# Squares of layer 0's norm on GpSimd, a new head of the program with constant dummies: a two-layer hybrid decoder trunk on one core

## The chip, the cores and the metric

One core of one Trainium2 chip. The metric is the device time of one execution in microseconds (us), the median of the runs. The engines are named as in the profile: PE (TensorE matmul), PEld (its weight loads), DVE (VectorE), ACT (ScalarE), POOL (GpSimd), SP (SyncE, which here issues nearly all DMAs). A name with a q behind it (ACTq, SPq) is the engine's instruction queue issuing a DMA.

## The reference, cut to what matters

Two layers over a sequence of 256 tokens of width 1024, batch 1, all in float32:

```python
def hybrid_layer(x, norm_w, w_in, ...):
    h = rmsnorm(x, norm_w)
    proj = jnp.matmul(h, w_in)          # 1024 -> 4360 columns
    ...                                  # attention (8 heads), retention (4), mLSTM (4), each gated
    y = jnp.concatenate([ya, yb, yc], axis=-1)
    return x + jnp.matmul(y, w_out)      # 1024 -> 1024
def reference(x, ...):
    for layer in range(2):
        x = hybrid_layer(x, ...)
    return rmsnorm(x, final_norm_w)
def rmsnorm(x, w):
    return x * lax.rsqrt(jnp.mean(x * x, axis=-1, keepdims=True) + 1e-6) * w
```

## The kernel before, in words

**Tiling.** x lies transposed in SBUF, width on the partitions: tile `px` holds 8 blocks (k = 0 to 7) of 128 partitions x 256 tokens, and beside them the small parameters. Float32 products are made from split operands: every operand is split into a high part (`hi`, `xh`: a copy of type fp32r) and a low part (`lo`, `xl`: the operand minus its high part), and each product takes three matmuls, high x high, high x low, low x high. The high part of a weight chunk is an ACT copy, the low part a DVE subtraction; for x (`split_x`, L431) the high part is an ACT copy scaled by the norm weight, the low part a DVE scalar_tensor_tensor. `xh` and `xl` lie in one tile, `xx`. The norm's 1/rms is not applied to x but to the results, when they leave PSUM.

**Staging.** The weights of a layer come in 21 chunks through three buffers of `raw`, `hi` and `lo` each (in the listings of an engine's order these are raw_85 to raw_87, hi_88 to hi_90, lo_91 to lo_93). Chunks 0 and 1 (`aq0`, `ak0`) are worked on together, block by block: for each k the matmuls are high/low of `xx` block k with both chunks, 12 matmuls per k, 4 groups of three; those 32 groups are the first real work of PE. `loader` (L390) issues their pieces on SP in the order x block, weight pieces, with five cuts of k (0; 1; 2, 3; 4, 5; 6, 7); the pieces of chunk 0 for k = 0 and k = 1 (the list `early`, L364) are issued on ACT's queue instead.

**Order of the work.** The kernel's own planner (`Sched`) sets each engine's order: every operation has an engine and a cost in the planner's clock, and what can start first is emitted first. Each engine then runs its list strictly in that order, waiting for semaphores where an operand isn't there. A `("act", 507.0, ...)` request is planned as ACT's work whatever engine its function really uses.

**The head of the program** (L359 to L377), emitted in front of everything the planner emits: DVE fills `ones`; ACT's queue issues the two early DMAs and then runs one Exp, in front of which the compiler puts the load of ACT's function table; DVE fills `mhalf`; POOL fills `va`, `vc`, `cpad` and the four padded tiles `zu` and `zd`; DVE zeroes a tile of `sb`, and PE runs two matmuls of 384 columns on it whose result nobody reads (dummies).

**The norm of a layer** (`norm`, L481): four Square operations on ACT, each over two blocks of x (128x512), into tiles `t`, summed by DVE; then a matmul with `ones` sums over the partitions, and POOL raises to the power -0.5. For layer 0 the third and fourth of these DVE sums stand in front of and between the low parts of the weight chunk 2, and the first one (`t_94<-t_94,t_95`) among the low parts of chunks 0 and 1.

Lines: L259 is every DVE operation, L265 every ACT operation of the planner, L280 every matmul, L288 every DMA that SP issues; they are told apart by tiles.

Of the kernel before, what the change touches and what calls it, by code (L numbers as in the profile page):

```python
# [55 lines left out]
W_TOTAL = W_OFFS[-1]  # L56


P_NW, P_CW, P_CB, P_GB, P_YW = 0, 16, 48, 56, 72
P_N = 72 + 8  # L60

T_ID, T_DIST, T_COS, T_SIN, T_QS, T_MC, T_DEC = 0, 128, 512, 768, 1024, 1028, 1412
T_1 = 1028
# [165 lines left out]
def trunk(ctx: ExitStack, tc: tile.TileContext, xp: bass.AP, w: bass.AP, fn: bass.AP,  # L229
# [7 lines left out]
    def sb_tile(shape, name, dt=F32):  # L237
        return cp.tile(shape, dt, name=name)
# [22 lines left out]
    def A(out, in_, func, after=None, table=False, **k):  # L261
        cost = _n(out) / 1.2 + 80 + 93 * sum(isap(v) for v in k.values())
        if func == AF.Ln or table:
            cost += 1283
        return op("act", cost, lambda: nc.scalar.activation(out, in_, func, **k), after)  # L265
# [21 lines left out]
    def D(cost, out, in_):  # L287
        return op("sp", cost, lambda: nc.sync.dma_start(out, in_))  # L288
# [14 lines left out]
        return wait(ev)  # L303


    px = sb_tile([128, P_N + KT * S], "px")
    pr = px[:, :P_N]
    x = px[:, P_N:].rearrange("p (k t) -> p k t", t=S)
    tb = sb_tile([128, T_N], "tb")
    ident = tb[:, T_ID:T_ID + 128]  # L310
    ones = sb_tile([128, 2], "ones")
# [44 lines left out]
    sc.pool("pj", [pp.tile([128, 512], F32, name=f"pj{i}") for i in range(4)])  # L356
    sc.pool("mx", [pp.tile([128, 512], F32, name=f"mx{i}") for i in range(4)])

    nc.vector.memset(ones, 1.0)  # L359

    early = []
    for k in range(2):
        d = slice(k * 256, (k + 1) * 256)
        early.append(nc.scalar.dma_start(sc.pools["raw"][0][0][0][:, d], w[:, d]))  # L364
    nc.scalar.activation(ones[:, 1:2], ones[:, 0:1], AF.Exp)
    nc.vector.memset(mhalf, -0.5)
    nc.gpsimd.memset(va, 1.0)
    nc.gpsimd.memset(vc, 1.0)
    nc.gpsimd.memset(cpad, 0.0)

    for tag, half in (("zu", slice(64, 128)), ("zd", slice(0, 64))):
        for t, _ in sc.pools[tag][0]:
            nc.gpsimd.memset(t[half].bitcast(F32), 0.0)
    dummy = sc.pools["sb"][0][0][0]
    nc.vector.memset(dummy, 0.0)
    for _ in range(2):
        nc.tensor.matmul(sc.pools["mx"][0][3][0][:, :384], dummy[:, :128], dummy, start=True, stop=True)  # L377

    evs = {}

# [9 lines left out]
    def loader():  # L390
        for i in range(NL):
            l, c = divmod(i, NW)
            n = W_SIZES[c]
            o = l * W_TOTAL + W_OFFS[c]
            if i == 1:
                continue
            t = yield acq("raw")
            raws[i] = t
            if i < 2:
                if i == 0:  # L400
                    t1 = yield acq("raw")
                    raws[1] = t1
                    for a, b in ((0, 1), (1, 2), (2, 4), (4, 6), (6, 8)):
                        o1, o2 = P_N + a * S if a else 0, P_N + b * S
                        e = yield D((o2 - o1) * 512 / 360.0, px[:, o1:o2], xp[:, o1:o2])
                        for k in range(a, b):
                            sc.set(E("x0", k), e + 1100)
                        for m in range(2):
                            if m == 0 and b <= 2:
                                e = yield op("sp", 364, lambda: early[a])  # L410
                            else:
                                e = yield D((b - a) * 364, (t, t1)[m][:, a * 256:b * 256],
                                            w[:, o + m * 2048 + a * 256:o + m * 2048 + b * 256])
                            for k in range(a, b):
                                sc.set(E("rawk", m, k), e + 1100)
                continue
            m = 2 if i == 2 else 1
            for j in range(m):
                a, b = j * n // m, (j + 1) * n // m
                e = yield D((b - a) * 512 / 360.0, t[:, a:b], w[:, o + a:o + b])  # L420
                for q in range(2 * j // m, 2 * (j + 1) // m):
                    sc.set(E("raw", i, q), e + 1100)
            if i == 2:
                e = yield D(1500, tb[:, :T_1], tab[:, :T_1])
                sc.set(E("tab"), e + 1100)
            if i == 4:
                e = yield D(3500, tb[:, T_1:], tab[:, T_1:])
                sc.set(E("tab2"), e + 1100)
        sc.spawn(last_in(), 2)

    def split_x(l, k):  # L431
        wk = pr[:, P_NW + l * 8 + k:P_NW + l * 8 + k + 1]
        yield A(xh[:, k, :], x[:, k, :], AF.Copy, scale=wk)
        t = yield V("scalar_tensor_tensor", xl[:, k, :], x[:, k, :], wk, xh[:, k, :].bitcast(F32),
                    op0=OP.mult, op1=OP.subtract)
        sc.set(E("x", l, k), t)
# [44 lines left out]
    def norm(l):  # L481

        ss = None
        for k in range(0, KT, 2):
            for z in (k, k + 1):
                yield wait(E("x0", z) if l == 0 else E("res", l - 1, z))
            sq = yield acq("t512")
            yield A(sq, x[:, k:k + 2, :].rearrange("p a t -> p (a t)"), AF.Square)
            if ss is None:
                ss = sq  # L490
            else:
                e = yield V("tensor_tensor", ss, ss, sq, op=OP.add)
                sc.release("t512", sq, e)
# [729 lines left out]
```

## Time and profile before

| | |
|---|---|
| time, median of 3 runs | 300.46 us (300.12 to 301.92) |
| the profiled execution, its own time | 299.76 us |
| its span, first to last instruction | 298.0 us |
| what lies around the span in it | 1.76 us |
| mean granted TensorE clock | 0.994 |
| busy: PE, DVE, ACT, POOL | 290.7, 257.9, 197.8, 13.7 us |

A row of a timeline gives the start (us from the span's start), the busy time, the engine, the line, the operation with its output and inputs, and how many instructions are merged in the row; in brackets the idle time before it and what ended it. Times of the matmuls' ends are modelled, so PE's pace is read from the distances between starts.

### The profile page before, as it was taken

The page shows a single profiled execution, that of the slowest core. Times are in us where ns is not written, and L with a number is a line of the kernel's source. Part 1 is how long each engine was busy: PE and PEld are TensorE (multiplying, and loading weights), DVE is VectorE, ACT ScalarE, POOL GpSimd, SP SyncE. Part 2 cuts the span into 40 slices and gives each one's busy share as a digit, 9 for nine tenths or more (in the row PEclk, how much of TensorE's full clock was granted, in tenths as well). Part 3 has the DMA queues.
Part 4 walks back from the last instruction along what each step waited for, and adds up shares of the span by engine and source line. Part 5 has one row for each costly group of instructions (what it writes and reads, how often), then busy time and mean ns, then how long its engine had stood idle before and what let it go on. Part 6 is the DMA issues. An engine that isn't in the chain of part 4 may idle for free.

```text
span 298.0 us, 4797 instructions
## 1 busy us (share of the span) xinstructions
PE 290.7 (98%) x1792; PEld 258.3 (87%) x1792; DVE 257.9 (87%) x551; ACT 197.8 (66%) x344; POOL 13.7 (5%) x17
## 2 busy tenths in 40 slices
PE   7999999999999999999999999999999999999992
PEld 5998999888989888899988888988899988888882
DVE  4969999999999997885779999999999999956553
ACT  7948997889358439644565799779555265745533
POOL 6000000000002002000020000000002002000000
PEclk9999999999999999999999999999999999999997
DMA  7999455664800560745317663446541624340003
GB/s 243 398 400 326 141 196 206 192 232 141 274 11 3 170 251 8 265 153 157 128 21 263 211 218 130 152 144 211 213 143 34 250 59 166 122 148 0 2 4 137
DMA packets 9095, 48.58 MB, mean 163 GB/s; under 512 B 1008, under 2 KB 1904, under 8 KB 4080
## 3 DMA queue, kind: packets, MB, share of 16 engines
q1 hardware_dynamic: 8784, 48.02, 46.4%
q8 instruction: 14, 0.23, 0.3%
q10 hardware_dynamic: 288, 0.26, 0.3%
q14 instruction: 9, 0.07, 0.1%
HBM read 47.23 MB, written 1.05 MB: 162 GB/s over the span
## 4 chain that ended last, share of the span: by engine, by line
PE 87%; DVE 9%; DMA 1%; ACT 1%; issue 1%; DVEq 0%
PE pj L280 69%; PE mx L280 14%; PE mx L285 4%; DVE lo L259 3%; DVE t L259 1%; DVE st L259 1%; DVE small L259 1%; DMA px<-xp 1%; DVE hc L259 1%; DVE sb L259 1%; DVE raw L259 1%; DVE et L259 0%; ACT raw L265 0%; DVE zd L259 0%; DVE zu L259 0%
## 5 line engine op out<-in xcount | busy, mean ns | idle before, releaser
L259 DVE TENSOR_TENSOR lo<-raw,hi 128x1024 fp32r<-128x1024 f32 (+2 forms) x96 | 102.7, 1087 | 7.9 <-ACT hi L265 7.7
L265 ACT ACTIVATE hi<-raw 128x1024 fp32r<-128x1024 f32 (+2 forms) x96 | 88.5, 946 | 9.7 <-DMA raw<-w 3.8
L280 PE MATMUL pj<-hi,xx 128*128 128x512 f32 (+1 forms) x320 | 94.3, 373 | 0.0
L280 PE MATMUL pj<-xx,hi 128*128 128x512 f32 (+1 forms) x272 | 88.0, 377 | 0.1
L280 PE MATMUL pj<-xx,lo 128*128 128x256 f32 x240 | 68.7, 286 | 0.0
L280 PEld LDWEIGHTS pj<-hi,xx 128*128 128x128 f32 x320 | 57.4, 188 | 9.0
L280 PE MATMUL pj<-lo,xx 128*128 128x512 f32 (+1 forms) x160 | 59.4, 371 | 0.0
L280 PEld LDWEIGHTS pj<-xx,hi 128*128 128x128 f32 x272 | 50.2, 194 | 9.6 <-ACT hi L265 1.3
L280 PEld LDWEIGHTS pj<-xx,lo 128*128 128x128 f32 x240 | 46.0, 192 | 0.1
L280 PEld LDWEIGHTS pj<-lo,xx 128*128 128x128 f32 x160 | 30.1, 188 | 4.5
L265 ACT ACTIVATE sb<-sb,small 128x128 f32<-128x128 f32 (+1 forms) x48 | 19.5, 449 | 4.9 <-DVE small L259 2.4
L265 ACT ACTIVATE t<-pj 128x256 f32<-128x256 f32 x26 | 9.8, 378 | 17.0 <-PE pj L280 16.9
L265 ACT ACTIVATE st<-t 64x512 fp32r<-64x512 f32 x26 | 16.1, 628 | 4.5 <-DVE t L259 4.1
L280 PE MATMUL pj<-yh,lo 128*128 128x256 f32 x56 | 15.9, 284 | 0.0
L280 PE MATMUL pj<-yh,hi 128*128 128x256 f32 x56 | 15.9, 284 | 0.0
L280 PE MATMUL pj<-yl,hi 128*128 128x256 f32 x56 | 15.8, 283 | 0.0
L1109 POOL TENSOR_TENSOR small<-small,mhalf 128x8 f32<-128x8 f32 x4 | 6.9, 1730 | 181.7 <-DVE small L259 181.7
L280 PE MATMUL mx<-st,st 128*128 128x128 f32 (+1 forms) x64 | 15.1, 270 | 0.0
L265 ACT ACTIVATE t<-pj,small 128x512 f32<-128x512 f32 (+1 forms) x12 | 7.3, 610 | 11.2 <-PE pj L280 11.1
L259 DVE TENSOR_TENSOR t<-pj,t 128x256 f32<-128x256 f32 x26 | 10.9, 419 | 2.2 <-ACT t L265 2.1
L265 ACT ACTIVATE t<-t 32x512 f32<-32x512 f32 (+1 forms) x20 | 12.6, 630 | 0.3
L280 PEld LDWEIGHTS mx<-st,st 128*128 128x128 f32 x64 | 12.1, 189 | 0.6
(151 smaller groups left out, 480.4 us busy)
## 6 DMA issues: line engine op xcount, KB each, us to landing
raw<-w SPq DMA_DIRECT2D x37, 1024.0 KB, 4.8
raw<-w SPq DMA_DIRECT2D x2, 1056.0 KB, 6.3
raw<-w SPq DMA_DIRECT2D x6, 256.0 KB, 5.0
raw<-w SPq DMA_DIRECT2D x2, 512.0 KB, 6.6
tb<-tab SPq DMA_DIRECT2D x1, 960.0 KB, 10.1
px<-xp SPq DMA_DIRECT2D x3, 256.0 KB, 4.3
tb<-tab SPq DMA_DIRECT2D x1, 514.0 KB, 7.5
raw<-fn SPq DMA_DIRECT2D x1, 512.0 KB, 3.2
```

The source lines that it names most:

```text
L259: return op("dve", cost, lambda: getattr(nc.vector, name)(out, *a, **k), after)
L265: return op("act", cost, lambda: nc.scalar.activation(out, in_, func, **k), after)
L280: return op("pe", cost, lambda: nc.tensor.matmul(out, a, b, start=start, stop=stop, skip_group_check=True), after)
L285: return op("pe", 110.0, lambda: nc.tensor.transpose(out, in_, idn))
L1109: yield G(1600, lambda: nc.gpsimd.tensor_tensor(vs, vs, mhalf[:, :8], op=OP.pow))
```

## The change

Six edits, all in the head of the program and in layer 0.

1. The four Squares of layer 0's norm become products x*x on POOL (`tensor_tensor`); the planner still books them as ACT's work of 507 ns. Layer 1 keeps ACT.
2. The high part of x block 0 in layer 0 (one 128x256 operation) goes from ACT to DVE (`tensor_scalar`); the planner still books it as ACT's.
3. The Exp that brings ACT's function table stands in front of ACT's two early DMA issues.
4. PE's dummies: eight matmuls of 128 columns on the constant zero tile that the framework fills at the program's start, in place of two of 384 columns on a tile that DVE zeroes. They stand at the top of the head.
5. POOL fills only the columns of `va`, `vc` and `cpad` that nothing else writes.
6. In `px` the norm weights (16 columns) lie in front of x and the other parameters behind it, so the first DMA of x has 272 columns in place of 336 and the last one 576 in place of 512.

```diff
@@ -56,8 +56,9 @@
 W_TOTAL = W_OFFS[-1]
 
 
-P_NW, P_CW, P_CB, P_GB, P_YW = 0, 16, 48, 56, 72
-P_N = 72 + 8
+P_NW, P_X = 0, 16
+P_CW = P_X + KT * S
+P_CB, P_GB, P_YW, P_N = P_CW + 32, P_CW + 40, P_CW + 56, P_CW + 64
 
 T_ID, T_DIST, T_COS, T_SIN, T_QS, T_MC, T_DEC = 0, 128, 512, 768, 1024, 1028, 1412
 T_1 = 1028
@@ -303,9 +304,9 @@
         return wait(ev)
 
 
-    px = sb_tile([128, P_N + KT * S], "px")
-    pr = px[:, :P_N]
-    x = px[:, P_N:].rearrange("p (k t) -> p k t", t=S)
+
+    pr = px = sb_tile([128, P_N], "px")
+    x = px[:, P_X:P_CW].rearrange("p (k t) -> p k t", t=S)
     tb = sb_tile([128, T_N], "tb")
     ident = tb[:, T_ID:T_ID + 128]
     ones = sb_tile([128, 2], "ones")
@@ -356,25 +357,23 @@
     sc.pool("pj", [pp.tile([128, 512], F32, name=f"pj{i}") for i in range(4)])
     sc.pool("mx", [pp.tile([128, 512], F32, name=f"mx{i}") for i in range(4)])
 
+    zero = nc.const_aps.tensor(0.0, (128, 128), F32)
+    for _ in range(8):
+        nc.tensor.matmul(sc.pools["mx"][0][3][0][:, :128], zero, zero, start=True, stop=True)
     nc.vector.memset(ones, 1.0)
+    nc.scalar.activation(ones[:, 1:2], ones[:, 0:1], AF.Exp)
 
     early = []
     for k in range(2):
         d = slice(k * 256, (k + 1) * 256)
         early.append(nc.scalar.dma_start(sc.pools["raw"][0][0][0][:, d], w[:, d]))
-    nc.scalar.activation(ones[:, 1:2], ones[:, 0:1], AF.Exp)
     nc.vector.memset(mhalf, -0.5)
-    nc.gpsimd.memset(va, 1.0)
-    nc.gpsimd.memset(vc, 1.0)
-    nc.gpsimd.memset(cpad, 0.0)
-
+    nc.gpsimd.memset(va[:, :, :, HD:], 1.0)
+    nc.gpsimd.memset(vc[:, :, :, HD:], 1.0)
+    nc.gpsimd.memset(cpad[:, :, :3], 0.0)
     for tag, half in (("zu", slice(64, 128)), ("zd", slice(0, 64))):
         for t, _ in sc.pools[tag][0]:
             nc.gpsimd.memset(t[half].bitcast(F32), 0.0)
-    dummy = sc.pools["sb"][0][0][0]
-    nc.vector.memset(dummy, 0.0)
-    for _ in range(2):
-        nc.tensor.matmul(sc.pools["mx"][0][3][0][:, :384], dummy[:, :128], dummy, start=True, stop=True)
 
     evs = {}
 
@@ -401,8 +400,8 @@
                     t1 = yield acq("raw")
                     raws[1] = t1
                     for a, b in ((0, 1), (1, 2), (2, 4), (4, 6), (6, 8)):
-                        o1, o2 = P_N + a * S if a else 0, P_N + b * S
-                        e = yield D((o2 - o1) * 512 / 360.0, px[:, o1:o2], xp[:, o1:o2])
+                        o1, o2 = P_X + a * S if a else 0, P_X + b * S if b < KT else P_N
+                        e = yield D(((b - a) * S + 80 * (a == 0)) * 512 / 360.0, px[:, o1:o2], xp[:, o1:o2])
                         for k in range(a, b):
                             sc.set(E("x0", k), e + 1100)
                         for m in range(2):
@@ -430,7 +429,10 @@
 
     def split_x(l, k):
         wk = pr[:, P_NW + l * 8 + k:P_NW + l * 8 + k + 1]
-        yield A(xh[:, k, :], x[:, k, :], AF.Copy, scale=wk)
+        if l + k:
+            yield A(xh[:, k, :], x[:, k, :], AF.Copy, scale=wk)
+        else:
+            yield op("act", 386.0, lambda: nc.vector.tensor_scalar(xh[:, k, :], x[:, k, :], wk, None, op0=OP.mult))
         t = yield V("scalar_tensor_tensor", xl[:, k, :], x[:, k, :], wk, xh[:, k, :].bitcast(F32),
                     op0=OP.mult, op1=OP.subtract)
         sc.set(E("x", l, k), t)
@@ -485,7 +487,12 @@
             for z in (k, k + 1):
                 yield wait(E("x0", z) if l == 0 else E("res", l - 1, z))
             sq = yield acq("t512")
-            yield A(sq, x[:, k:k + 2, :].rearrange("p a t -> p (a t)"), AF.Square)
+            xk = x[:, k:k + 2, :].rearrange("p a t -> p (a t)")
+            if l:
+                yield A(sq, xk, AF.Square)
+            else:
+
+                yield op("act", 507.0, lambda: nc.gpsimd.tensor_tensor(sq, xk, xk, op=OP.mult))
             if ss is None:
                 ss = sq
             else:
@@ -1211,7 +1218,8 @@
         par[:, P_YW + 4 * l:P_YW + 4 * l + 2] = f(ret_norm_w)[l].reshape(2, 128).T
         par[:, P_YW + 4 * l + 2:P_YW + 4 * l + 4] = f(mlstm_norm_w)[l].reshape(2, 128).T
     fn = np.ascontiguousarray(np.broadcast_to(f(final_norm_w), (128, D_)))
-    ins = {"xp": np.concatenate([par, xT], 1), "w": w, "fn": fn, "tab": _tables()}
+    par[:, P_X:P_CW] = xT
+    ins = {"xp": par, "w": w, "fn": fn, "tab": _tables()}
 
     nc = _bacc.Bacc("TRN2", target_bir_lowering=False, num_devices=1)
     args = [nc.dram_tensor(n, a.shape, mybir.dt.from_np(a.dtype), kind="ExternalInput").ap() for n, a in ins.items()]
```

What the scheduler makes of it, per engine. ACT's list from the program's start; raw_85 and hi_88 belong to chunk 0, raw_86 and hi_89 to chunk 1, `t_94` and `t_95` hold the squares, `xx<-px` is the high part of x. Before:

```order
L364 DMA raw_85<-w 128x256 x2
L365 ACT_TABLE_LOAD
L365 ACTIVATE ones<-ones 128x1
L265 ACTIVATE xx<-px 128x256
L265 ACTIVATE hi_88<-raw_85 128x256
L265 ACTIVATE hi_89<-raw_86 128x256
L265 ACTIVATE xx<-px 128x256
L265 ACTIVATE hi_88<-raw_85 128x256
L265 ACTIVATE t_94<-px 128x512
L265 ACTIVATE hi_89<-raw_86 128x256
```

and with the change:

```order
L364 ACT_TABLE_LOAD
L364 ACTIVATE ones<-ones 128x1
L369 DMA raw_85<-w 128x256 x2
L266 ACTIVATE hi_88<-raw_85 128x256
L266 ACTIVATE hi_89<-raw_86 128x256
L266 ACTIVATE xx<-px 128x256
L266 ACTIVATE hi_88<-raw_85 128x256
L266 ACTIVATE hi_89<-raw_86 128x256
```

The two DMA issues moved behind the table load and the Exp; the first high part of x and the square are gone from the list; the rest stands in the same order.

DVE's list from the program's start, where lo_91 and lo_92 are the low parts of chunks 0 and 1, before:

```order
L375 MEMSET sb_111 128x384
L259 SCALAR_TENSOR_TENSOR xx<-px,xx 128x256
L259 TENSOR_TENSOR lo_91<-raw_85,hi_88 128x256
L259 TENSOR_TENSOR lo_92<-raw_86,hi_89 128x256
```

and with the change, down to the first sum of squares:

```order
L435 TENSOR_SCALAR xx<-px 128x256
L260 SCALAR_TENSOR_TENSOR xx<-px,xx 128x256
L260 TENSOR_TENSOR lo_91<-raw_85,hi_88 128x256
L260 TENSOR_TENSOR lo_92<-raw_86,hi_89 128x256
L260 SCALAR_TENSOR_TENSOR xx<-px,xx 128x256
L260 TENSOR_TENSOR lo_91<-raw_85,hi_88 128x256
L260 TENSOR_TENSOR lo_92<-raw_86,hi_89 128x256
L260 SCALAR_TENSOR_TENSOR xx<-px,xx 128x256 x2
L260 TENSOR_TENSOR lo_91<-raw_85,hi_88 128x256 x2
L260 TENSOR_TENSOR t_94<-t_94,t_95 128x512
L260 TENSOR_TENSOR lo_92<-raw_86,hi_89 128x256 x2
```

The fill of `sb` gave its place to the high part of x block 0; the sum of the first two squares stands where it stood, behind lo_91 of k = 2, 3 and in front of lo_92 of the same blocks.

## Rows read from the trace of the kernel before

**Rows 1.** The chain of work that ended last, its shares by engine, from the page.

```profile
PE 87%; DVE 9%; DMA 1%; ACT 1%; issue 1%; DVEq 0%
```

**Rows 2.** Busy time of each engine in stretches of the span. Columns: the stretch, its length, then busy us (and instructions) of PE, PEld, DVE, ACT, POOL, the granted clock, the DMA engines' share, GB/s.

```profile
4.00:6.00 2.00, 1.87 (x7) 1.53 (x7) 1.85 (x5) 1.92 (x6) 1.09 (x3) 1.00 1.05 316
8.00:10.00 2.00, 2.00 (x19) 2.00 (x18) 2.00 (x6) 2.00 (x6) 0.00 (x0) 1.00 1.00 361
...
260.00:280.00 20.00, 20.00 (x116) 17.33 (x114) 13.41 (x23) 11.48 (x18) 0.00 (x0) 1.00 0.19 69
```

**Rows 3.** Timeline of PE from the start: the dummies (L377), then the groups of three of chunks 0 and 1.

```profile
1.38 2.93 PE L377 MATMUL mx<-sb 128*128 128x384 f32 x4 [1.38 <-DVE sb L375]
4.43 0.80 PE L280 MATMUL pj<-xx,hi 128*128 128x256 f32 x2
5.03 0.54 PE L280 MATMUL pj<-xx,lo 128*128 128x256 f32 x1
5.36 0.63 PE L280 MATMUL pj<-xx,hi 128*128 128x256 f32 x2
...
6.00 0.63 PE L280 MATMUL pj<-xx,hi 128*128 128x256 f32 x2
...
7.28 0.52 PE L280 MATMUL pj<-xx,hi 128*128 128x256 f32 x2
...
7.76 0.40 PE L280 MATMUL pj<-xx,hi 128*128 128x256 f32 x2
...
8.11 0.40 PE L280 MATMUL pj<-xx,hi 128*128 128x256 f32 x2
...
9.79 0.28 PE L280 MATMUL pj<-xx,lo 128*128 128x256 f32 x1
```

**Rows 4.** Timeline of ACT and its queue from the start.

```profile
0.73 0.89 ACTq L364 DMA_DIRECT2D raw<-w  x2
1.65 1.28 ACT L365 ACT_TABLE_LOAD   x1 [1.65 <-PEq L1216]
2.94 0.20 ACT L365 ACTIVATE ones<-ones 128x1 f32<-128x1 f32 x1
3.56 0.51 ACT L265 ACTIVATE xx<-px 128x256 fp32r<-128x256 f32 x1 [0.42 <-DMA px<-xp]
3.98 0.70 ACT L265 ACTIVATE hi<-raw 128x256 fp32r<-128x256 f32 x2
...
5.48 0.61 ACT L265 ACTIVATE t<-px 128x512 f32<-128x512 f32 x1
...
6.42 0.91 ACT L265 ACTIVATE xx<-px 128x256 fp32r<-128x256 f32 x2
```

**Rows 5.** DMA issues of the first 24 us: what they move, the queue, how many, KB each, median us from issue to landing.

```profile
raw<-w ACTq DMA_DIRECT2D x2, 128.0 KB, 3.1
px<-xp SPq DMA_DIRECT2D x1, 168.0 KB, 2.8
```

**Rows 6.** Timeline of DVE: the head, the low parts around the first sum of squares, and two scalar multiplications at the end of the program.

```profile
0.80 0.06 DVE L359 MEMSET ones<- 128x2 f32 x1 [0.80 <-PEq L1216]
...
4.10 0.49 DVE L259 SCALAR_TENSOR_TENSOR xx<-px,xx 128x256 fp32r<-128x256 f32 x1 [2.79 <-ACT xx L265]
4.51 0.76 DVE L259 TENSOR_TENSOR lo<-raw,hi 128x256 fp32r<-128x256 f32 x2
...
6.44 0.43 DVE L259 TENSOR_TENSOR lo<-raw,hi 128x256 fp32r<-128x256 f32 x1 [0.31 <-ACT hi L265]
...
8.50 0.69 DVE L259 TENSOR_TENSOR t<-t,t 128x512 f32<-128x512 f32 x1
9.11 0.76 DVE L259 TENSOR_TENSOR lo<-raw,hi 128x256 fp32r<-128x256 f32 x2
...
292.38 0.15 DVE L259 TENSOR_SCALAR small<-small 128x1 f32<-128x1 f32 x1
...
293.96 0.42 DVE L259 TENSOR_SCALAR raw<-raw,small 128x384 f32<-128x384 f32 x1
```

**Rows 7.** Timeline of POOL.

```profile
0.34 0.10 POOL L1216 MEMSET const-uint8-127<- 128x1 uint8 x1
0.73 0.96 POOL L367 MEMSET va<- 128x1040 f32 x1 [0.29 <-POOLq L1216]
...
4.16 0.98 POOL L373 MEMSET zd<- 64x512 f32 x2
20.44 0.70 POOL L502 TENSOR_TENSOR small<-small,mhalf 128x2 f32<-128x2 f32 x1 [15.29 <-DVE small L259]
...
247.79 2.00 POOL L1109 TENSOR_TENSOR small<-small,mhalf 128x8 f32<-128x8 f32 x1 [20.36 <-DVE small L259]
```

**Rows 8.** POOL's groups, costliest first: line, operation, shapes, how many | busy us, mean ns of one | idle before.

```profile
L1109 POOL TENSOR_TENSOR small<-small,mhalf 128x8 f32<-128x8 f32 x4 | 6.9, 1730 | 181.7 <-DVE small L259 181.7
...
L369 POOL MEMSET cpad<- 128x1036 f32 x1 | 1.0, 965 | 0.0
...
L368 POOL MEMSET vc<- 128x520 f32 x1 | 0.5, 531 | 0.0
```

**Rows 9.** Timelines of DVE and PE where chunk 3 comes in (`lo` of its first half, its first matmuls).

```profile
21.02 1.23 DVE L259 TENSOR_TENSOR lo<-raw,hi 128x1024 fp32r<-128x1024 f32 x1 [0.74 <-ACT hi L265]
...
23.96 0.27 PE L280 MATMUL mx<-xx,lo 128*128 128x256 f32 x1
```

## The prediction

> **What bounds the kernel now.** I read four views. First the chain of work that ended last: 87% of it is PE [rows 1]; the reader is to see that what any other engine does counts only where PE waits for it. Second the stretches of the span: PE is busy for all of each stretch, at the front (8 to 10) as near the end (260 to 280) [rows 2]. So a time by which PE's stream of matmuls is moved at the head arrives at the end, and work taken from ACT or DVE without moving PE is worth nothing. Third PE's timeline at the head, read by starts [rows 3]: dummies from 1.38, the first real matmul at 4.43, waiting for a high part, the next group of three at 5.36. From there groups follow each other without a hole, 0.64 apart (5.36 to 6.00, and 6.00 to 7.28 holds two), later 0.35 to 0.36 apart (7.76 to 8.11). [...] Fourth the timelines of ACT, DVE and POOL up to 10 us, to see who is late there. Both ACT and DVE are full from 8 to 10 [rows 2], but PE has what it needs: its tightest place is the low part of chunk 1 for k = 2, which DVE ends at 9.11 + 0.42 = 9.53 and PE takes at 9.79, so 0.26 of slack, the least I find [rows 3, 6]. Later it is larger: the first half of chunk 3's low part ends at 22.25 and is used at 23.96 [rows 9].
>
> The profiled execution took 299.76 us, 1.76 around its span of 298.0. The median of the runs is 300.46, which is 0.70 above it. I sum against the 299.76 and add 0.70 at the end. About 1% (3.0 us) is what a measurement of this kernel can tell from no change.
>
> **The change, part by part.**
>
> *ACT's table load in front of its DMA issues.* Before, the two issues run from 0.73 to 1.62 and the table load starts at 1.65, takes 1.28, and the Exp follows to 3.14; ACT then still idles 0.42 until x has landed [rows 4]. So the table load is not late now, and the move gains nothing there. What it may cost: the issues carry chunk 0's weights for k = 0 and 1, and every first matmul waits for them. If the queue passes the Exp only when the Exp starts, they go out at 0.73 + 1.28 + 0.02 = 2.03; if it doesn't wait, after the fill of `ones` that the Exp needs (0.80 + 0.06), at about 0.95. No row shows a DMA issue behind a table load. I take the waiting end, because the one row of the kind, the table load that begins 0.03 behind the second issue though its engine had been idle since 0, shows the queue taking its entries one after the other. From issue to landing I take 2.8, the shortest in the rows, since the ring of SP is already flowing by then (3.1 is ACT's own) [rows 5]: landing at 4.83 in place of about 3.75. The high part is started at 3.98 before, and the first matmul comes 0.45 later [rows 3, 4]; with the change 4.85 + 0.45 = 5.30. The low part needs the high part and 0.42 more, so the third matmul comes at about 5.75 in place of 5.03, and the second group about 0.7 late. Bounds: -0.2 (not held) to +0.9.
>
> What 0.7 is worth: PE is then at the half pace, 0.64 per group; the groups not done are done later at 0.36, so 0.7 x 0.36 / 0.64 = **+0.4 us** (bounds -0.1 to +0.5).
>
> *The first high part of x on DVE.* ACT takes 0.51 for it [rows 4]; on DVE a scalar multiplication of 1 column takes 0.15 and of 384 columns 0.42 [rows 6], so 256 take about 0.33. x lands at 3.54 and its first DMA is a fifth smaller; the low part can start at about 3.9 in place of 4.10. Hidden behind the weights, which land later: **0**. Were the weights not late, it would save up to 0.3.
>
> *The dummies.* Four passes of 384 columns took 2.93, 0.73 each [rows 3]; sixteen of 128 columns at a third of that, 0.24, take 3.9, from 0.75 (no DVE fill to wait for) to about 4.65. That is before 5.30, so they hold up nothing; a pass would have to take 0.28. They start 0.6 earlier. If the rise of the clock comes as much earlier, that is worth 0.6 x (1 - 0.36 / 0.64) = -0.26. But the hole between dummies and real work grows from under 0.5 to 0.65 or more, and if the rise goes by the real work (0.87 later), it costs 0.87 x 0.44 = +0.38. Between ends of both signs I take **0**.
>
> *Squares on POOL.* ACT loses four operations of 0.61 [rows 4], about 2.1 with their overlap. PE waits for none; DVE's 0.31 of idle behind the late high part (6.13 to 6.44) goes [rows 6], which adds to PE's slack only: **0**. On POOL they are new. For the length of one: at least 0.5, as a fill of 512 columns (0.96 for 1040); at most, by its multiplications, powers of 8 columns, 1.73 on the mean and 2.00 the longest [rows 7, 8]; a power of 512 columns has no row and would be far longer. I take 1.7. The first can start by 5.48 at the latest, when ACT squared the same blocks, the second at 6.42, when the blocks 2 and 3 are there (ACT starts on them then [rows 4]); and the first, begun when block 1 lands, is then nearly done; so the second ends at about 8.1. DVE adds the two at 8.50 [rows 6]. So it is covered by 0.4, and by 0.26 more at PE. Every further us of delay would be a us at PE, because the low part of chunk 1 for k = 2 is queued behind that sum on DVE. The other two squares have until 14 us.
>
> *The shorter fills* take about 2.2 from POOL: 0.96, 0.53 and 0.97 become about 0.1 each, as the fill of a constant takes; the fills end at 2.9 in place of 4.16 + 0.98 = 5.14 [rows 7, 8]. Nobody waits for them before: **0**, but they open the way for the squares. *The smaller first DMA* (32 KB of 168) brings x earlier by about 0.1, hidden by the weights: **0**. The parameters that now come last are needed only by the convolution, long after.
>
> **Sum:** +0.4. 299.76 + 0.4 + 0.70 = 300.9 us.
>
> **The rivals.**
>
> *A, ACT's issues are not held.* Then the first matmul starts at about 4.2 (weights 3.75 + 0.45) in place of 4.43, worth -0.1, and with dummies that begin earlier and run nearly into the real work the clock's -0.26: 299.76 - 0.4 + 0.70 = 300.1. More can't come, since beyond 0.3 to 0.5 the low part of k = 2 stops PE. For it: the table load is work of the engine, not of its queue. Against it: the 0.03. [...]
>
> *B, POOL starts late; the side of slower.* Mechanism: DVE runs strictly in order, the sum of the first two squares stands in front of the low part that PE needs at 9.79 [rows 3, 6]. Before, 15.3 us pass between POOL's last fill and its first TENSOR_TENSOR [rows 7], so anything POOL needs to get ready for that kind was hidden. Now fills end at about 2.9. If getting ready takes p, the second square ends at 2.9 + p + 2 x 1.7, and what is over 8.8 is lost: it decides from p = 2.5. The trace bounds p by 0 and 15.3; at 6.2, the geometric middle between 2.5 and 15.3, the loss is 3.7 and the time 300.9 + 3.7 = 304.6. Against it: the power at 20.44 took 0.70, the shortest of its kind. [...]
>
> *C, POOL slows DVE.* Where a two-input operation of DVE runs beside a square it might take up to twice as long. Two squares lie in front of 9.5, 3.4 us; DVE would lose up to 1.7, less 0.26 of slack and 0.4 that PE is late itself: +1.0, so 301.9. Against it: beside POOL's fills a DVE operation took 0.49 at 4.10 and no more than that later [rows 6, 7], but fills read nothing.
>
> **How the numbers follow.** Forecast 0.55, A 0.22, C 0.13, B 0.10. The forecast's 300.9 has its own bounds of -0.5 and +0.4 and a scatter of the runs of about 0.7 around it. The range runs from 299.5 (A, with half a us of scatter) to 302.7 (C, with the same), and leaves B out. Faster by over 1% has no case, 0.01; slower by over 1% (above 303.5) is most of B, 0.08; within 1% is the rest, 0.91.
>
> **What would show it.** Right: ACT's two issues begin near 2.0, the first high part of chunk 0 ends past 5, PE's first real matmul is near 5.3, the second group about 0.7 late; POOL's squares take under 2 and the DVE sum doesn't wait. A: issues near 0.9, first matmul near 4.2. B: an idle time on DVE before the first sum that names POOL, and a hole in PE near 9. C: subtractions of 256 columns that take more than 0.42 beside squares. The forecast is wrong if the pace of the groups rises at a time far from 7.5, or if PE waits anywhere behind 10 us where it did not before.

## The result and the profile after

| | before | changed |
|---|---|---|
| time, median of 8 runs each, taken together | 300.19 us (299.80 to 301.92) | 302.87 us (301.69 to 303.42) |
| ratio | | 1.0077, 95% interval 1.0060 to 1.0094 |
| the profiled execution: its time, its span | 299.76, 298.0 us | 303.27, 301.5 us |

The change costs 2.3 us by the ratio, 2.7 by the medians. That is less than the 1% (3.0 us) that the prediction takes as its bound, but the interval of the ratio lies wholly on the slower side. 300.9 was forecast; the measured median is 0.17 above the top of the range. The three runs that the forecast starts from had a median 0.27 above that of these eight, so measured from 300.19 the miss is larger: +2.7 in place of +0.4.

ACT's head in the changed kernel, against [rows 4]:

```profile
0.72 1.28 ACT L364 ACT_TABLE_LOAD   x1 [0.72 <-PEq L1224]
0.90 0.87 ACTq L369 DMA_DIRECT2D raw<-w  x2
2.02 0.20 ACT L364 ACTIVATE ones<-ones 128x1 f32<-128x1 f32 x1
3.48 0.79 ACT L266 ACTIVATE hi<-raw 128x256 fp32r<-128x256 f32 x2 [1.26 <-DMA raw<-w]
```

The issues are not held: they go out at 0.90, while the table is being loaded (0.72 to 2.00). The first high part starts at 3.48 in place of 3.98.

PE in the changed kernel, against [rows 3]; two stretches of its timeline:

```profile
0.77 3.75 PE L362 MATMUL mx<-const-float32-0.0 128*128 128x128 f32 x16 [0.77 <-PEq L1224]
4.17 0.77 PE L281 MATMUL pj<-xx,hi 128*128 128x256 f32 x2
...
4.96 0.62 PE L281 MATMUL pj<-xx,hi 128*128 128x256 f32 x2
...
8.69 0.54 PE L281 MATMUL pj<-xx,hi 128*128 128x256 f32 x2 [0.47 <-ACT hi L266]
9.57 0.39 PE L281 MATMUL pj<-xx,lo 128*128 128x256 f32 x1 [0.35 <-DVE lo L260]
...
11.69 0.39 PE L281 MATMUL pj<-xx,lo 128*128 128x256 f32 x1 [1.15 <-DVE lo L260]
11.91 0.40 PE L281 MATMUL pj<-xx,hi 128*128 128x256 f32 x2
...
12.27 0.61 PE L281 MATMUL pj<-xx,hi 128*128 128x256 f32 x2
...
12.89 0.63 PE L281 MATMUL pj<-xx,hi 128*128 128x256 f32 x2
...
15.91 0.40 PE L281 MATMUL pj<-xx,hi 128*128 128x256 f32 x2
...
20.59 0.40 PE L281 MATMUL pj<-xx,hi 128*128 128x256 f32 x2
```

The first real matmul comes 0.26 earlier than before. Then PE stands still three times (a stretch in which it does is called a hole here), the last time for 1.15 us in front of the low part of chunk 1 for k = 2. One step behind that hole the groups of three are 0.62 to 0.64 apart again (12.27 to 12.89, and so on to 15.45), and the stretches print a granted clock of 0.57 and 0.58 there (columns as in [rows 2]); this drop is called the fall of the clock below:

```profile
10.00:12.00 2.00, 0.85 (x7) 0.65 (x6) 2.00 (x4) 2.00 (x8) 1.13 (x2) 1.00 1.04 377
12.00:14.00 2.00, 2.00 (x13) 2.00 (x12) 2.00 (x4) 1.88 (x6) 0.87 (x1) 0.57 1.03 417
14.00:16.00 2.00, 2.00 (x12) 2.00 (x12) 2.00 (x7) 1.26 (x2) 0.00 (x0) 0.58 0.88 353
```

At the start of the kernel before the column prints 1.00 beside groups 0.64 apart (5.36 to 7.28). So the slow pace of the start, and its end, which the prediction and the expectations call the rise of the clock, can be read from the distances alone, and that it is the same thing as this fall is not shown.

Why the low part came late stands on DVE, here beside POOL, against [rows 6, 7]:

```profile
5.51 0.85 DVE L260 SCALAR_TENSOR_TENSOR xx<-px,xx 128x256 fp32r<-128x256 f32 x1 [0.79 <-ACT xx L266]
...
9.77 1.52 DVE L260 TENSOR_TENSOR t<-t,t 128x512 f32<-128x512 f32 x1
11.22 0.75 DVE L260 TENSOR_TENSOR lo<-raw,hi 128x256 fp32r<-128x256 f32 x2
```

```profile
5.04 1.04 POOL L495 TENSOR_TENSOR t<-px 128x512 f32<-128x512 f32 x1 [2.05 <-DMA px<-xp]
7.46 1.04 POOL L495 TENSOR_TENSOR t<-px 128x512 f32<-128x512 f32 x1 [1.38 <-DMA px<-xp]
9.54 1.21 POOL L495 TENSOR_TENSOR t<-px 128x512 f32<-128x512 f32 x1 [1.04 <-DMA px<-xp]
11.62 1.25 POOL L495 TENSOR_TENSOR t<-px 128x512 f32<-128x512 f32 x1 [0.87 <-DMA px<-xp]
```

The first sum takes 1.52 in place of 0.69, and nobody is named in front of it: it doesn't wait for the squares it adds (they ended at 6.08 and 8.50). It runs beside the third one, which ends at 9.54 + 1.21 = 10.75, and ends 0.54 behind that. The scaled subtraction at 5.51 (0.85 in place of 0.49) ends at 6.36, 0.28 behind the first square's 6.08. So each seems to be held until POOL's operation is over. Four later profiles bear it out: in the changed kernel's second one, e2, e3 and f2 this subtraction begins 0.36 to 0.47 into the first product, and each time it ends 0.28 behind the product's end.

From the start of group 32, the last of chunks 0 and 1, to the end of the span it is 280.9 us in both kernels (17.11 of 298.0, 20.59 of 301.5). The whole difference arises in the first 21 us.

### The profile page after: what moved, and what is told of

Same layout as the page of the kernel before. It is cut to its first block, busy times and chain, and to the rows that moved or that the text cites. A ratio compares the mean times of both kernels' runs of the same rounds, so it can differ in the third digit from the quotient of the medians.

```text
span 301.5 us, 4826 instructions
## 1 busy us (share of the span) xinstructions
PE 292.9 (97%) x1804; PEld 261.5 (87%) x1804; DVE 260.3 (86%) x551; ACT 195.9 (65%) x339; POOL 17.0 (6%) x21
## 4 chain that ended last, share of the span: by engine, by line
PE 85%; DVE 9%; DMA 3%; issue 1%; ACT 0%; SPq 0%; DVEq 0%
PE pj L281 67%; PE mx L281 14%; PE mx L286 4%; DMA raw<-w 3%; DVE lo L260 3%; DVE t L260 1%; DVE st L260 1%; DVE small L260 1%; DVE hc L260 1%; DVE sb L260 1%; DVE raw L260 1%; DVE et L260 0%; SPq L289 0%; ACT raw L266 0%; DVE zd L260 0%
## 5 line engine op out<-in xcount | busy, mean ns | idle before, releaser
L281 PE MATMUL pj<-xx,hi 128*128 128x512 f32 (+1 forms) x272 | 89.0, 381 | 0.5 <-ACT hi L266 0.5
L281 PEld LDWEIGHTS pj<-xx,hi 128*128 128x128 f32 x272 | 50.9, 196 | 9.0 <-ACT hi L266 0.7
L266 ACT ACTIVATE t<-t 32x512 f32<-32x512 f32 (+1 forms) x20 | 12.6, 629 | 0.3
L281 PEld LDWEIGHTS mx<-st,st 128*128 128x128 f32 x64 | 12.1, 189 | 0.6
```

Source lines behind the costliest of these rows:

```text
L281: return op("pe", cost, lambda: nc.tensor.matmul(out, a, b, start=start, stop=stop, skip_group_check=True), after)
```

## The experiments

**Theory P:** squares on POOL hold DVE's operations of two inputs; their low parts come late, PE stands still, and its clock may fall back. **Theory D:** what costs is that the weights land late. In the first profiles the pieces of k = 2 and later landed about 1 us behind those of before, and the theory's reason is that ACT's issues now stand behind SP's first ones, which holds SP's ninth and later issues. The ninth goes out at 4.89 in place of 4.60, behind a wait of 0.5 for a DMA of x; that the order of the issues or of the semaphores brings this wait is the author's estimate, which no run shows.

All profiles together, from PE's timeline, the spans and the DMA issues (start plus time to landing). Groups are the groups of three of [rows 3], counted from the first real matmul; the columns give their starts. Group 12 is the one behind the low part of chunk 1 for k = 2; the last column is the landing of x blocks 2 and 3. The landings, spans and groups are of one execution each.

| kernel | median, ratio [95%] | group 1 | group 12 | group 32 | span | x 2, 3 |
|---|---|---|---|---|---|---|
| before | 300.19 | 4.43 | 9.91 | 17.11 | 298.0 | 6.4 |
| before, second profile | 300.25 (one run) | 4.35 | 10.38 | 17.57 | 298.5 | 6.5 |
| changed | 302.87, 1.0077 | 4.17 | 11.91 | 20.59 | 301.5 | 7.4 |
| changed, second profile | 301.38 (one run) | 4.17 | 11.43 | 18.77 | 299.6 | 6.9 |
| e1, squares on ACT | 300.30, 1.0008 [0.9998, 1.0017] | 4.18 | 10.36 | 17.55 | 298.5 | 6.8 |
| e2, before + squares on POOL | 301.56, 1.0048 [1.0031, 1.0064] | 4.53 | 10.72 | 18.85 | 299.8 | 6.7 |
| e3, issues first | 302.72, 1.0078 [1.0052, 1.0103] | 4.17 | 11.37 | 18.71 | 299.6 | 6.8 |
| e4, both | 300.29, 0.9998 [0.9987, 1.0009] | 4.06 | 10.32 | 17.52 | 298.4 | 6.9 |
| f2, before + idle products | 301.59, 1.0052 [1.0035, 1.0069] | 4.45 | 11.79 | 19.08 | 299.9 | 7.2 |
| f3, before + idle one-input | 300.39, 1.0014 [1.0004, 1.0025] | 4.37 | 10.84 | 18.02 | 298.9 | 6.7 |
| g1, before, sum behind | 299.85, 0.9985 [0.9972, 0.9998] | 4.38 | 10.28 | 17.47 | 298.3 | 7.2 |
| g4, e4, sum behind | 300.25, 0.9995 [0.9980, 1.0010] | 4.18 | 10.16 | 17.34 | 298.5 | 7.0 |
| g5, squares in four | 301.87, 1.0051 [1.0033, 1.0068] | 4.17 | 11.27 | 18.46 | 299.5 | 6.9 |

**e1: squares back on ACT.**

```diff
-            if l:
+            if True:
                 yield A(sq, xk, AF.Square)
```

> The changed kernel with one edit undone: the four squares of layer 0's norm are ACT's again, everything else as changed. Theory P (products on POOL stretch DVE's two-input operations beside them, so low parts come late, PE stands still and its clock falls back): DVE's first sum takes 0.7 again in place of 1.52, PE has no hole of over 0.5 us behind 8 us, no stretch with a granted clock near 0.5 before 20 us, and the time falls to 299.3 to 300.0, since the earlier rise of the clock (5.5 in place of 7.5) then stays as a gain. Theory D (the weights land about 1 us later because ACT's issues now stand behind SP's in the order of the DMA semaphores, which holds SP's later issues): the landings stay late, PE keeps its holes, and the time stays at 302 to 303.

Measured 300.30: the loss is gone, as P has it. From group 12 to group 32 (10.36 to 17.55) the groups are 0.36 apart, and the sum takes its old length again:

```profile
9.05 0.69 DVE L260 TENSOR_TENSOR t<-t,t 128x512 f32<-128x512 f32 x1
```

PE still stands still for 0.52 until 8.23, waiting for a high part, and for 0.26 in front of the low part of chunk 1. The gain is not there: 299.3 to 300.0 was expected.

**e2: before, with squares on POOL.** The edit is the change's own, in `norm` alone.

```diff
-            yield A(sq, x[:, k:k + 2, :].rearrange("p a t -> p (a t)"), AF.Square)
+            xk = x[:, k:k + 2, :].rearrange("p a t -> p (a t)")
+            if l:
+                yield A(sq, xk, AF.Square)
+            else:
+                yield op("act", 507.0, lambda: nc.gpsimd.tensor_tensor(sq, xk, xk, op=OP.mult))
```

> The kernel before with one edit done: the four squares of layer 0's norm as products on POOL, everything else as before. Theory P: the first sum on DVE takes about 1.5 in place of 0.69, the low part of chunk 1 for k = 2 comes 0.8 or more late, 0.26 of it is slack; PE gets a hole of 0.5 to 1.2 us near 10 us, and if that makes the clock fall back as in the changed kernel 1.5 more: 300.8 to 303. Theory D: nothing that PE waits for moves, 300.0 to 300.4.

Measured 301.56, P. DVE there, and the POOL operation beside it:

```profile
9.44 0.67 DVE L259 TENSOR_TENSOR t<-t,t 128x512 f32<-128x512 f32 x1
10.04 0.74 DVE L259 TENSOR_TENSOR lo<-raw,hi 128x256 fp32r<-128x256 f32 x2
10.71 2.50 DVE L259 SCALAR_TENSOR_TENSOR xx<-px,xx 128x256 fp32r<-128x256 f32 x2
```

```profile
9.27 2.42 POOL L492 TENSOR_TENSOR t<-px 128x512 f32<-128x512 f32 x1 [1.50 <-DMA px<-xp]
```

```profile
10.50 0.39 PE L280 MATMUL pj<-xx,lo 128*128 128x256 f32 x1 [0.30 <-DVE lo L259]
...
13.60 0.39 PE L280 MATMUL pj<-xx,lo 128*128 128x256 f32 x1 [0.69 <-DVE lo L259]
```

This time the sum kept its length and the square took 2.42 in place of 1.04: POOL was the one held, while DVE's sum and two low parts ran. The two subtractions that followed took 2.50 for 0.88 and ran into the rest of this square and into the next one. So the larger hole of PE comes behind them, at 13.60, and not near 10. The expected place of the loss was wrong, its size right. The order in which they begin does not settle which of the two is held: here POOL's product begins at 9.27, inside a low part of DVE (9.10 to 9.51), and is held; in the changed kernel the third one begins inside two low parts as well (9.54, in 9.10 to 9.85), and the sum behind them is held. Why POOL did not get in between these operations of DVE, as it does behind the sum in f2 below, is open.

**e3: ACT's issues in front of the table load again**, POOL keeps the squares.

```diff
-    nc.scalar.activation(ones[:, 1:2], ones[:, 0:1], AF.Exp)
     early = []
     for k in range(2):
         ...
+    nc.scalar.activation(ones[:, 1:2], ones[:, 0:1], AF.Exp)
```

> The changed kernel with one edit undone: ACT issues its two early DMAs in front of the table load and the Exp again; squares stay on POOL. Theory P: the stretched sum stays (about 1.5), PE's hole and the fall of its clock stay, 302 to 303. Theory D: SP's issues go out as before (the ninth near 4.6 in place of 4.9 to 5.7), the pieces of k = 2, 3 land near 6.4, 7.1 and 7.7 in place of 7.4, 8.2 and 8.8, PE has no hole behind 8 us, and the time is 299.3 to 300.2.

Measured 302.72, all of the loss still there, so the order of the issues is not the cause. The pieces of x and weights stayed late too (x blocks 2 and 3 at 6.8, 6.4 in the first profile of before), so this run alone doesn't separate late landings from P. e1 does: there they are as late (6.8), and the loss is gone. D falls as the main cause.

**e4: both undone**, by the two edits of e1 and e3.

> The changed kernel with two edits undone: squares on ACT and ACT's issues in front of the table load; the dummies, x block 0's high part on DVE, the short fills and the new layout of px stay. Both theories: no loss left, and the clock's earlier rise stays: 299.3 to 300.0. If both causes have a part, this is faster than each with one undone alone; a time above 300.4 would say that something else (layout, dummies, the high part on DVE) costs as well.

Measured 300.29, the same as before. So the other five edits together (e1), and four of them with the issues as before (e4), bring nothing that these runs can tell from 0.

**Second profiles of before and of the changed kernel.**

> The kernel before, profiled a second time. In the four experiments so far the weights of k = 2 and later landed 0.3 to 0.8 us later than in the profile of before, whichever edit was undone. If that comes of the new head (layout, dummies), this profile shows the landings of the first one: the second piece of chunk 1 at 5.5, the third of x at 6.4, the last pieces at 12.1. If it differs from one execution to the next, they are late here too, by 0.3 or more, and PE's pace may rise at another time than 7.5. Time 299.8 to 300.6.

> The changed kernel, profiled a second time. Theory P: each DVE operation of two inputs that meets a square on POOL ends later by up to a square's length, and where PE then stands still its clock may fall back; the fall is worth 1.5 by the profile of the changed kernel (six groups at 0.64 in place of 0.36). A profile without the fall would show 301.3 to 302, one with it 302.6 to 303.5. Rival (late landings only): the first sum on DVE takes 0.7 and the holes of PE name DMA or ACT.

In the second profile of before x blocks 2 and 3 land near where they did, but chunk 1's last piece lands at 12.9 in place of 12.1, as in the experiments (12.6 to 13.2 in e1 to e4). And x blocks 2 and 3, issued at 2.56 to 2.58 everywhere, land at 6.4 to 7.2 with the old head and at 6.8 to 7.4 with the new one. So the landings differ mostly from one execution to the next, and D's premise was one early profile set beside one late one. With it goes the slack that the prediction read there. PE in the second profile of before:

```profile
10.16 0.39 PE L280 MATMUL pj<-xx,lo 128*128 128x256 f32 x1 [0.25 <-DVE lo L259]
```

Where [rows 3, 6] had 0.26 to spare, PE stands still for 0.25. The second profile of the changed kernel has no fall of the clock at the head (the column prints 1.00 from 8 to 16) and takes 301.38; DVE and POOL there:

```profile
9.30 0.68 DVE L260 TENSOR_TENSOR t<-t,t 128x512 f32<-128x512 f32 x1
9.90 1.59 DVE L260 TENSOR_TENSOR lo<-raw,hi 128x256 fp32r<-128x256 f32 x2
```

```profile
9.67 1.20 POOL L495 TENSOR_TENSOR t<-px 128x512 f32<-128x512 f32 x1 [1.65 <-DMA px<-xp]
```

Now it is the low parts that are held (1.59 for 0.76), to the same effect at PE:

```profile
11.21 0.39 PE L281 MATMUL pj<-xx,lo 128*128 128x256 f32 x1 [1.14 <-DVE lo L260]
11.43 0.40 PE L281 MATMUL pj<-xx,hi 128*128 128x256 f32 x2
...
11.79 0.40 PE L281 MATMUL pj<-xx,hi 128*128 128x256 f32 x2
```

The hole is as long, but the groups go on 0.36 apart. What the fall costs in the first profile: six steps from 12.27 to 15.91 take 3.64 in place of 6 x 0.36 = 2.16, so 1.5 us. Of the eight runs of the changed kernel five have a mean granted clock of 0.989 or 0.990 and take 302.86 to 303.42; the other three have 0.995 to 0.999 and take 301.69 to 302.62. The mean alone is a rough sign, because the clock also drops at the end of some executions: the first profile of before has 0.71 from 293 to 296, 0.50 from there to 297.8 and 1.00 in front of them, and a mean of 0.994. So a run at 0.995 may have a fall at the head or not; one at 0.990 or less has, as far as these traces go, both. Two of e3's four runs are at 0.989 (303.04 and 303.26), none of e2's and f2's eight is under 0.994, and of the 61 runs of before that were taken beside the experiments one is, 302.29 at 0.990. Why kernels with the new head show the sign more often than e2 and f2 is not shown.

**f2 and f3: idle work on POOL, in the kernel before.** ACT keeps the squares; nobody waits for POOL.

The line of f2 comes first, that of f3 in its place second; the loop around it, which waits for two blocks of x each time, is left out.

```diff
...
+            yield op("pool", 1040.0, lambda: nc.gpsimd.tensor_tensor(scr, xk, xk, op=OP.mult))
...
+            yield op("pool", 1040.0, lambda: nc.gpsimd.tensor_scalar(scr, xk, 2.0, None, op0=OP.mult))
...
```

> The kernel before, with four products x*x of 128x512 more on POOL, begun when their blocks of x land; they go to a place that nobody reads for a long time, and nobody waits for them; ACT still squares for the norm. Theory P, in the form that POOL and DVE exclude each other: DVE's two-input operations that meet a product take up to 1.04 longer and the product is itself held where it meets DVE's, the time goes up as with the squares themselves: 301.2 to 302. Rival (what costs is that DVE waits for the squares' result): 300.0 to 300.4.

Measured 301.59, as e2: the loss needs nobody to wait for the squares. Running beside them is enough. DVE, POOL and PE:

```profile
9.65 0.68 DVE L259 TENSOR_TENSOR t<-t,t 128x512 f32<-128x512 f32 x1
10.26 1.59 DVE L259 TENSOR_TENSOR lo<-raw,hi 128x256 fp32r<-128x256 f32 x2
```

```profile
9.82 1.41 POOL L1190 TENSOR_TENSOR on_a<-px 128x512 f32<-128x512 f32 x1 [1.44 <-DMA px<-xp]
```

```profile
11.57 0.39 PE L280 MATMUL pj<-xx,lo 128*128 128x256 f32 x1 [1.15 <-DVE lo L259]
```

> As the experiment with four idle products, but each is an operation with one tensor as input (x times 2, 128x512). If only operations with two tensors as inputs on both sides exclude each other, DVE's operations keep their lengths (0.42 and 0.69) and the time is 300.0 to 300.4. If any reading operation of POOL holds DVE, the lengths grow as with products and the time is 301 to 302.

Measured 300.39, at the upper end of the first expectation (300.0 to 300.4); the ratio's interval lies just above 1, so there is a small loss. POOL takes longer for one input (1.50 to 2.43), and DVE loses less. Beside the first of these operations DVE keeps its lengths (0.49 and 0.42 in [rows 6]):

```profile
5.75 0.51 DVE L259 SCALAR_TENSOR_TENSOR xx<-px,xx 128x256 fp32r<-128x256 f32 x1 [0.55 <-ACT xx L265]
6.19 0.41 DVE L259 TENSOR_TENSOR lo<-raw,hi 128x256 fp32r<-128x256 f32 x1
```

```profile
5.38 1.50 POOL L1190 TENSOR_SCALAR on_a<-px 128x512 f32<-128x512 f32 x1 [0.24 <-DMA px<-xp]
```

Beside the third it loses some time:

```profile
9.73 1.17 DVE L259 TENSOR_TENSOR lo<-raw,hi 128x256 fp32r<-128x256 f32 x2
```

```profile
9.40 1.77 POOL L1190 TENSOR_SCALAR on_a<-px 128x512 f32<-128x512 f32 x1 [0.73 <-DMA px<-xp]
```

Two low parts that begin 0.33 into an operation of 1.77 lose 0.41, and they are over at 10.90, before POOL is at 11.17. So an operation of one input does not keep DVE out to its end, as a product does. What the 0.41 is lost to is open.

**g1 and g4: the first sum behind the low parts**, in before and in e4.

In `first_w` the low part of chunk 1 for k = 3 is now followed by the sum that `norm` has put aside. The two places:

```diff
+            if m and k == 3:
+                held.pop()()
...
+                e = yield op("dve", 602.3, (lambda: held.append(add)) if l + k == 2 else add)
```

> The kernel before with one thing moved on DVE: the first sum of squares, which stands in front of the low parts of chunk 1 for k = 2 and 3, is issued right behind them. The second profile of before shows PE 0.25 idle there for that low part and the twelfth group of three at 10.38. Theory (PE's head is bounded at this place by DVE's list, whatever the head does before): the idle time of 0.25 goes, the twelfth group comes at about 10.1 and the time falls by 0.2 to 0.4, to 299.7 to 299.9. Rival (the place is not tight on the median, the landings are): no change, 300.0 to 300.2.

> The experiment with squares on ACT and ACT's DMA issues in front of the table load, with the first sum moved behind the low parts of chunk 1 for k = 2 and 3 as well: new dummies, high part of x block 0 on DVE, short fills and layout as in the changed kernel. By the theory that DVE's list at this place swallows what the head brings, the head's gain (the first group 0.2 earlier, the clock's rise up to 2 earlier) now reaches further: 299.3 to 299.8, ahead of the kernel before with the same move by 0.1 to 0.4. Rival (the weights' landings bound it): the same time as the kernel before with the same move, within 0.1.

g1 measured 299.85, 0.15% faster than before by an interval that just leaves out 1, and the lowest median of all kernels run: PE no longer waits for DVE there, and its group 12 is at 10.28. In g4 group 12 is at 10.16, 0.12 ahead of g1 as expected, but the median is 300.25. That is over the 299.3 to 299.8 that were expected and 0.4 above g1's, where the rival allowed 0.1. In these two profiles the 0.12 are still there at group 32 (17.34 and 17.47) and are lost behind it. Why stays open.

**g5: each square in four.**

```diff
-                yield op("act", 507.0, lambda: nc.gpsimd.tensor_tensor(sq, xk, xk, op=OP.mult))
+                def pieces():
+                    for q in range(0, 512, 128):
+                        i = nc.gpsimd.tensor_tensor(sq[:, q:q + 128], xk[:, q:q + 128], xk[:, q:q + 128], op=OP.mult)
+                    return i
+                yield op("act", 507.0, pieces)
```

> The changed kernel with each square on POOL cut into four operations of 128x128. If one operation holds the other engine for its whole length and no longer, a DVE operation of two inputs is now held by a quarter of 1.04, and no low part or sum takes more than about 0.4 over its own length; PE's hole near 10 shrinks from 1.15 to about 0.5, the clock does not fall back, and the time is 300.5 to 301.5. If the two engines share by bandwidth, or POOL gets the next piece in at once and DVE waits for all four, the loss stays: 301.5 to 303.

Measured 301.87, 1.0 us less than the changed kernel. That is 0.4 over the expected range and lies in the rival's (301.5 to 303), so the time doesn't decide; the lengths do. DVE and PE:

```profile
9.57 0.88 DVE L260 TENSOR_TENSOR t<-t,t 128x512 f32<-128x512 f32 x1
10.37 1.16 DVE L260 TENSOR_TENSOR lo<-raw,hi 128x256 fp32r<-128x256 f32 x2
```

```profile
11.04 0.39 PE L281 MATMUL pj<-xx,lo 128*128 128x256 f32 x1 [0.90 <-DVE lo L260]
```

The sum takes 0.88 (1.52 in the changed kernel, 0.69 alone), and each low part loses 0.2. So DVE isn't kept waiting for all four pieces; a hold of one instruction of POOL fits. But the pieces take turns with DVE's operations for 6.5 us (twelve in 6.48, 0.54 each), so DVE loses 0.1 to 0.2 some dozen times, and PE still has a hole of 0.90, where about 0.5 was expected.

## Why the prediction came out as it did

**That only the head counts** held: from group 32 to the end it is 280.8 to 281.2 us in all thirteen profiles.

**"Squares on POOL: 0" is the step that failed.** Its working asked only when the squares end, against the sum that waits for them, and there it was safe: 1.04 to 1.25 each, not 1.7, and the second one ended at 8.50, with the sum starting at 9.77. What it left at zero is what a square does to DVE beside it; the runs show 1.1 to 1.6 us there. In the changed kernel it was the third square, of which the prediction only says that it has until 14 us. That is rival C, at a chance of 0.13. The runs bear out its mechanism, and in most profiles its place, in front of the low part for k = 2 (in e2 the larger hole is at 13.60). That its 301.9 lies near e2's 301.56 and f2's 301.59 is in part luck: it has two squares of 1.7 slow DVE to half speed, where the squares took 1.04 to 1.25 and one of them held the sum for 0.83. That the forecast had the right side, slower, is luck as well: its +0.4 is a different term, which the runs don't show, and the loss came out of one that it put at 0. C was set low for the reason that a DVE operation beside POOL's fills kept its length (0.49); but fills read nothing, as the prediction itself says ([rows 7] show no input for them), so that row could not speak against it. C's form was off as well: in the traces DVE isn't slowed to half, it ends 0.28 to 0.54 behind POOL's operation (changed kernel), or POOL is the one held (2.42 for 1.04 in e2). The prediction's own signs of being wrong came: PE waits behind 10 us (until 11.69), and the pace first rises at 5.5 and not near 7.5.

Beside products the changed kernel has DVE's operations at 0.85 and 1.52, in place of 0.49 and 0.69 before, and they end 0.28 and 0.54 behind POOL's end; in e2 POOL was kept out over three operations of DVE. Beside POOL's operation of one input it is otherwise: in f3 DVE lost nothing to speak of beside the first (0.51 and 0.41 for 0.49 and 0.42), and 0.41 beside the third, where it finished before POOL (10.90 against 11.17). What the two engines share, and what decides which of them is held, no run shows.

**"ACT's table load in front of its DMA issues: +0.4" was wrong too**, and rival A right: issues at 0.90, first matmul at 4.17 (A: near 0.9 and 4.2). The 0.03 in [rows 4] had told of the program's order and not of a table load that holds the queue. In the changed kernel the DMAs at 0.90 went out beside a table load of 0.72 to 2.00. But A's gain of 0.4 isn't there either: e1 has that head without POOL's squares, e4 the same with ACT's issues in front again, and they measure 300.30 and 300.29 against 300.14 for before, taken beside them. Group 1 comes 0.2 to 0.4 earlier there, and group 12 at 10.36 and 10.32, where the second profile of before has 10.38. The low part for k = 2 is behind x blocks 2 and 3, which land at 6.4 to 7.4 whatever ACT and PE do at the head, and behind the sum. That PE swallows what it has won at this place was in A's text as a limit; that nothing at all is left was not.

**The dummies: 0** is not contradicted, but no run has the dummies alone: e1 and e4 show 0 for them together with other edits. The first two groups that are 0.36 apart start at 5.1 (g1) to 7.8 us (before) with the old dummies, and at 4.9 (e4) to 6.8 us (second profile of the changed kernel) with the new ones: the rise of the pace differs more between executions than between the two kinds of dummies. Whether it goes by the dummies or by the real work, the two cases that the prediction's -0.26 (a term of A's 300.1 as well) and +0.38 stand for, no run shows; what the runs show is the start of the faster pace, at 4.9 to 7.8.

**The slack of 0.26** was read from one execution. In the second one PE waited 0.25 there.

**Rival B** did not come: POOL's first square began at 5.04, when its blocks had landed, and the sum waited for none. POOL had been free since 2.99, and the profile puts the 2.05 between down to the DMA of x; so getting ready, if it was part of them, took no more than 2.05, under the 2.5 from which the prediction lets it decide.

**The size.** C alone is worth 1.1 to 1.6 us: 301.38 in the profile without a fall of the clock, e2 and f2. The prediction named no fall. By the mean clock it happens in most runs of the changed kernel, and in the one profile that has it it costs 1.5. Together that is 2.6 to 3.1, against a measured 2.7. This is an estimate and not a measurement: no run has the fall alone, and a run of e3 at 0.999, without it, still took 302.40.

## What to carry to other kernels

Before work goes from a busy engine to POOL, list what DVE does at that time: here its operations of two inputs were held beside POOL's products (the sum took 1.52 in place of 0.69 beside a product of 1.21), although no wait names it. The sign in these traces is a longer duration, not an idle time. A hole in PE of 1.15 cost more than its length where the clock fell back behind it (0.57, six steps in 3.64 in place of 2.16), as it did in one of the two profiles of the changed kernel. A slack of a quarter of a microsecond in the wake of DMAs is not a slack until a second profile shows it: the 0.26 to spare in the first profile of before was 0.25 of standing still in the second.

## What the runs showed of the hardware that was not expected

- DVE's operations of two inputs and POOL's products of two inputs held each other: DVE's 0.69 became 1.52 (changed kernel) and its 0.76 for two low parts became 1.59 (f2), ending 0.54 and 0.62 behind POOL's operation; POOL's 1.04 became 2.42 (e2).
- POOL's operation with one tensor input of 128x512 took 1.50 to 2.43 beside DVE (f3), the product with two took 1.04 to 1.41 in the same place (f2). The first of the former, 1.50 long, took no more than 0.03 from DVE's operations beside it.
- ACT's queue issued two DMAs at 0.90 while ACT's table load ran from 0.72 to 2.00 (changed kernel).
- In one profile of the changed kernel PE was busy 1.18 of 2.00 us from 8 to 10 and 0.85 from 10 to 12, with a hole of 1.15 until 11.69, and groups 0.62 to 0.64 apart at a granted clock of 0.57 followed from 12.27 on. In its other profile (1.65 and 0.86, a hole of 1.14) and in f2 (1.65 and 0.85, a hole of 1.15) none followed.
- The same piece of x, issued at 2.56 to 2.58, landed at 6.4 in one execution (before) and at 7.4 in another (changed).
